# Column means of an 8192 x 8192 matrix: the first pairs added whole, the last accumulation in parts, another order of matmuls and stores

## The chip, the core and the metric

The kernel runs on one core of a Trainium2 chip. The metric is the device time of one execution in microseconds, as a median over runs. Five engines matter. VectorE (DVE in the profile) adds, TensorE (PE) multiplies matrices, ScalarE (ACT) copies and issues some stores, GpSimd (POOL) sets constants, and SyncE (SP) issues the loads. Data moves between the chip's main memory (HBM) and the on-chip memory (SBUF) through 16 DMA engines. TensorE writes its sums into PSUM banks.

## The reference

```python
def setup_inputs():
    return {"x": np.random.randn(8192, 8192).astype(np.float32)}

def reference(x):
    return np.mean(x, axis=0)
```

The input is 268 MB and the output 32 KB. Every input element is read once and added into its column.

## The kernel before

The 8192 rows are cut into 64 groups of 128 rows. A group fills one buffer of 128 partitions by 8192 columns (`P` = 128, `N` = 8192). There are six such buffers in one tile, `bufs` (L29). Buffers 0 to 3 take loads; buffer 4 is called `both` and holds the sum of one pair of groups; buffer 5 is called `acc` and is the accumulator.

Groups are loaded in pairs, 8 MB per load (`load_rows`, L64). Each partition takes two neighbouring rows, so that one lies in buffer `u` and the other in `u + 1`. Group numbers below name a pair by its first group: "group 6" is the pair 6 and 7. Group 0 is loaded straight into `both` and `acc`. Groups 2, 6, 10 and so on go into buffers 0 and 1, groups 4, 8, 12 and so on into buffers 2 and 3 (`u = (g + 2) % 4`). Load 6 therefore has to wait until VectorE has read group 2, and load 8 until it has read group 4.

All loads are issued by SyncE in the order of the program (`load`, L50). A load's issue waits for the adds that read its buffers.

VectorE sums the groups. `add` (L69) issues one addition. Where an add needs a load, a no-op on ScalarE or GpSimd waits for the load and for the add before, and the add waits for the no-op (L74). The first add puts group 0 together (L85). In the loop from L87, each pair takes two adds of 8192 columns:

```python
    for g in range(2, G - 4, 2):
        u = (g + 2) % 4
        dma = load_rows(g, u, 2)
        add(both, bufs[:, u, :], bufs[:, u + 1, :], [dma])
        add(acc, acc, both, [])
```

The first of them is the only one that reads the loaded buffers. Group 60 is added straight into `acc` in three parts of the columns, 8, 4 and 4 blocks of 512 columns, with two adds to each part (L95 to L99).

Groups 62 and 63 are not added by VectorE. Group 62 is loaded in one piece (L101) and group 63 in four (L103), and TensorE reads them. `blocks` (L107) lists matmuls, one for each 512 columns of a row of blocks: `acc`, `r62` (group 62) and `r63` (group 63) are each multiplied with a matrix of ones over 8192, so that the 128 partitions are summed and the results of all three are added up in PSUM. Blocks 0 to 14 fill four banks, four blocks to a bank and three in the last; block 15 goes in four pieces into `last`. The calls from L116 to L123 set the order.

At the end ScalarE copies the four banks to `res` (a part of `both`), VectorE copies `last` to `tail` (L146), and three stores write the output: `s0` for banks 0 to 2 (issued by SyncE), `s3` for bank 3 (issued by ScalarE), and one for `tail` (issued by SyncE). `landed` (L44) makes SyncE wait for what it is given: ahead of `s0` for the waiters' no-ops, ahead of the last store for the loads, the fourth copy and the last matmul, and at the end for the stores.

Of the kernel before, what the change touches and what calls it, by code (L numbers as in the profile page):

```python
# [1 line left out]

# [4 lines left out]


@with_exitstack
def kernel(  # L10
    ctx: ExitStack,
    tc: tile.TileContext,
    x: bass.AP,
    out: bass.AP,
):
    nc = tc.nc
    f32 = mybir.dt.float32
    M, N = x.shape
    P = nc.NUM_PARTITIONS
    F = 512  # L20
    W = F // 4
    G = M // P
    U = 6
    sync = mybir.DependencyInfo(mybir.DependencyClass.Sync, mybir.DependencyReason.DATA)

    sb = ctx.enter_context(tc.tile_pool(name="sb", bufs=1))
    psp = ctx.enter_context(tc.tile_pool(name="psum", bufs=1, space=bass.MemoryType.PSUM))

    bufs = sb.tile([P, U, N], f32, name="bufs")  # L29
    both = bufs[:, U - 2, :]  # L30
    acc = bufs[:, U - 1, :]
    ones = sb.tile([P, 32], f32, name="ones")
    tail = sb.tile([P, W], f32, name="tail")
    warm = sb.tile([P, 32], f32, name="warm")
    nc.gpsimd.memset(ones[:], 1.0 / M)  # L35
    ready = sb.tile([P, 1], f32, name="ready")
    set_up = tc.keep_in_program_order(
        nc.gpsimd.tensor_add(out=ready[:], in0=ones[:, 0:1], in1=ones[:, 1:2])).ins  # L38
    banks = [psp.tile([P, F], f32, name=f"bank{b}") for b in range(4)]
    last = psp.tile([P, W], f32, name="last")  # L40

    loads = []

    def landed(*inss):  # L44

        nop = tc.keep_in_program_order(nc.sync.nop()).ins
        for o in inss:
            tc.add_manual_dep(nop, o.name, sync, reason="SyncE waits")

    def load(dst, src):  # L50
        ins = tc.keep_in_program_order(nc.sync.dma_start(out=dst, in_=src)).ins
        k = len(loads)
        over = loads[k - 8:k - 6] if k >= 8 and k % 2 == 0 else []
        tc.declare_no_dep(ins, group="loads", keep=over, reason="the reader of the buffer waited")
        for o in over:
            tc.add_manual_dep(ins, o.name, sync, reason="covers the next load too")
        tc.add_to_no_dep_group("loads", ins)
        loads.append(ins)
        return ins

    def rows(g, n=1):
        return x[g * P:(g + n) * P, :]

    def load_rows(g, u, n):  # L64
        return load(bufs[:, u:u + n, :], rows(g, n).rearrange("(p j) c -> p j c", j=n))

    adds, joins = [], {}

    def add(dst, a, b, dmas):  # L69

        ins = tc.keep_in_program_order(nc.vector.tensor_add(out=dst, in0=a, in1=b)).ins  # L71
        if dmas and adds:
            waiter = nc.scalar if len(adds) % 8 > 1 else nc.gpsimd
            nop = joins[waiter] = tc.keep_in_program_order(waiter.nop()).ins  # L74
            for o in dmas + adds[-1:]:
                tc.add_manual_dep(nop, o.name, sync, reason="the no-op waits")
            for group in ("loads", "adds"):
                tc.declare_no_dep(ins, group=group, reason="the no-op waited")
            tc.add_manual_dep(ins, nop.name, sync, reason="waits for both at once")
        elif adds:  # L80
            tc.declare_no_dep(ins, group="loads", reason="the add ahead waited")
        tc.add_to_no_dep_group("adds", ins)
        adds.append(ins)

    add(acc, acc, both, [load_rows(0, U - 2, 2)])  # L85
    tc.keep_in_program_order(nc.scalar.copy(out=warm[:], in_=ones[:]))  # L86
    for g in range(2, G - 4, 2):  # L87
        u = (g + 2) % 4
        dma = load_rows(g, u, 2)
        add(both, bufs[:, u, :], bufs[:, u + 1, :], [dma])  # L90
        add(acc, acc, both, [])

    u = (G - 4 + 2) % 4
    dma = [load_rows(G - 4, u, 2)]
    for lo, hi in [(0, 8), (8, 12), (12, 16)]:  # L95
        cols = slice(lo * F, hi * F)
        for j in range(2):
            add(acc[:, cols], acc[:, cols], bufs[:, u + j, cols], dma)
            dma = []  # L99
    r62, r63 = [bufs[:, 2 - u + j, :] for j in range(2)]  # L100
    load(r62, rows(G - 2))  # L101
    for lo, hi in [(0, 8), (8, 12), (12, 15), (15, 16)]:
        load(r63[:, lo * F:hi * F], rows(G - 1)[:, lo * F:hi * F])  # L103

    sums = []

    def blocks(row, lo, hi):  # L107
        for i in range(lo, hi):
            if i < 15:
                sums.append((banks[i // 4], i % 4, row[:, i * F:(i + 1) * F]))  # L110
            else:
                for q in range(4):
                    at = i * F + q * W
                    sums.append((last, q, row[:, at:at + W]))

    blocks(acc, 0, 8)  # L116
    blocks(r62, 0, 16)
    blocks(acc, 8, 12)
    blocks(r63, 0, 8)
    blocks(r63, 8, 12)  # L120
    blocks(acc, 12, 16)
    blocks(r63, 12, 15)
    blocks(r63, 15, 16)  # L123
    for n, (dst, q, cols) in enumerate(sums):
        summed = tc.keep_in_program_order(nc.tensor.matmul(  # L125
            out=dst[32 * q:32 * q + 32, :],
            lhsT=ones[:],
            rhs=cols,
            start=all((d is dst, k) != (True, q) for d, k, _ in sums[:n]),
            stop=all((d is dst, k) != (True, q) for d, k, _ in sums[n + 1:]),  # L130
            tile_position=(0, 32 * q),
            skip_group_check=True,
        )).ins

    res = both[:, :4 * F].rearrange("p (b c) -> p b c", b=4)

    def copy(dst, src):
        return tc.keep_in_program_order(nc.scalar.copy(out=dst, in_=src)).ins  # L138

    def store(engine, dst, src):  # L140
        return tc.keep_in_program_order(engine.dma_start(out=dst, in_=src)).ins

    for b in range(3):
        copy(res[:, b, :], banks[b][:])
    copied = copy(res[:96, 3, :], banks[3][:96])
    ended = nc.vector.tensor_copy(out=tail[:], in_=last[:]).ins  # L146
    landed(*joins.values())
    s0 = store(nc.sync, out[:12 * F].rearrange("(b q c) -> q b c", q=4, c=F), res[0:P:32, 0:3, :])
    s3 = store(nc.scalar, out[12 * F:15 * F].rearrange("(q c) -> q c", q=3), res[0:96:32, 3, :])
    landed(loads[-5], set_up)  # L150
    landed(*loads[-4:-2])
    landed(loads[-2], copied)
    landed(loads[-1], summed)
    store(nc.sync, out[15 * F:].rearrange("(q c) -> q c", q=4), tail[0:P:32, :])
    landed(s0, ended)
    landed(s3)
    hold = tc.keep_in_program_order(nc.vector.nop()).ins
    tc.add_manual_dep(hold, s0.name, sync, reason="VectorE ends late")


# [1 line left out]
_INS = ['x']  # L162
_OUTS = [((8192,), 'float32')]


# [23 lines left out]
```

## Time and profile before

| | us |
|---|---|
| median of three runs | 631.38 (631.07 to 631.54) |
| the profiled execution | 631.49 |
| its span, first to last instruction | 629.6 |
| VectorE busy | 531.0 |
| TensorE busy | 13.1 |
| HBM read over the span | 268.44 MB, 426 GB/s |

A line of the timeline has the start in us, the busy time, the engine, the source line, the operation, its output and input tiles with their shapes, how many there were, and in brackets how long the engine was idle before and what released it. "SPq" and "ACTq" are the queues of instructions of SyncE and ScalarE that are not counted as busy, such as issuing a transfer. "PEld" is the loading of weights into TensorE. A line of the chain of waits has a start, a duration and what it was. A line of the windows has the stretch, its length, the busy time and number of instructions of TensorE, weight loads, VectorE, ScalarE and GpSimd, then TensorE's granted clock, the DMA engines' busy share, and GB/s.

### The profile page before, as it was taken

To read this page: it belongs to the slowest core of one execution; us is meant where nothing else is said; L and a number is where in the kernel's file an instruction comes from. 1 tells how busy PE (TensorE), PEld (TensorE's weight loads), DVE (VectorE), ACT (ScalarE), POOL (GpSimd) and SP (SyncE) were. 2 spreads that over 40 slices of the span, in tenths; PEclk is the share of its full clock that TensorE was granted. 3 is DMA by queue.
4 is the path that set the end of the run, shared out by engine and by line. 5 is a ranking of instruction groups with operands and counts; after the bars stand their busy time and mean duration, and the time that the engine had idled before them with its cause. 6 is when DMAs were issued, how large, how long until landed. Compare 5 with 4: busy or idle time off the path is not lost.

```text
span 629.6 us, 442 instructions
## 1 busy us (share of the span) xinstructions
PE 13.1 (2%) x114; PEld 4.9 (1%) x114; DVE 531.0 (84%) x66; ACT 3.8 (1%) x6; POOL 0.5 (0%) x6
## 2 busy tenths in 40 slices
PE   0000000000000000000000000000000000000007
PEld 0000000000000000000000000000000000000002
DVE  0538988889988889888898888998888988889885
ACT  0000000000000000000000000000000000000001
POOL 0000000000000000000000000000000000000000
PEclk9999999999999999999999999999999999999999
DMA  9999999999999999999999999999999999999995
GB/s 400 408 458 421 446 441 425 446 421 454 412 454 412 454 412 458 408 462 404 462 404 462 404 462 404 462 404 462 404 463 404 462 404 462 404 462 404 462 392 214
DMA packets 5216, 268.50 MB, mean 426 GB/s; under 512 B 587, under 2 KB 591, under 8 KB 862
## 3 DMA queue, kind: packets, MB, share of 16 engines
q1 hardware_dynamic: 5208, 268.46, 98.7%
q8 instruction: 1, 0.02, 0.0%
q10 hardware_dynamic: 6, 0.01, 0.0%
q14 instruction: 1, 0.01, 0.0%
HBM read 268.44 MB, written 0.03 MB: 426 GB/s over the span
## 4 chain that ended last, share of the span: by engine, by line
DMA 67%; DVE 21%; another core or an unknown queue 9%; PE 2%; ACT 0%; issue 0%; ACTq 0%
DMA bufs<-in_x_dram 67%; DVE bufs L71 21%; PE bank L125 2%; ACT L86 0%; PE last L125 0%; ACT bufs L138 0%; ACTq L74 0%; ACT warm L86 0%
## 5 line engine op out<-in xcount | busy, mean ns | idle before, releaser
L71 DVE TENSOR_TENSOR bufs<-bufs 128x8192 f32<-128x8192 f32 (+2 forms) x65 | 530.7, 8167 | 91.4 <-ACTq L74 43.3
L125 PE MATMUL bank<-bufs,ones 128*32 128x512 f32 x90 | 12.8, 687 | 613.1 <-DVE bufs L71 613.1
L125 PEld LDWEIGHTS bank<-bufs,ones 128*32 128x32 f32 x90 | 4.2, 125 | 619.3 <-issue 618.2
L138 ACT COPY bufs<-bank 128x512 f32<-128x512 f32 (+1 forms) x4 | 2.3, 584 | 622.0 <-DMA bufs<-in_x_dram 620.2
L146 DVE COPY tail<-last 128x128 f32<-128x128 f32 x1 | 0.3, 292 | 4.2 <-PE bank L125 4.2
L125 PE MATMUL last<-bufs,ones 128*32 128x128 f32 x24 | 2.3, 276 | 0.0
L86 ACT ACT_TABLE_LOAD x1 | 1.3, 1283 | 0.7 <-PEq L173 0.7
L125 PEld LDWEIGHTS last<-bufs,ones 128*32 128x32 f32 x24 | 1.2, 110 | 1.7 <-issue 1.7
L86 ACT COPY warm<-ones 128x32 f32<-128x32 f32 x1 | 0.2, 218 | 0.0
L38 POOL TENSOR_TENSOR ready<-ones 128x1 f32<-128x1 f32 x1 | 0.2, 193 | 0.1
L35 POOL MEMSET ones<- 128x32 f32 x1 | 0.1, 124 | 0.3 <-POOLq L173 0.3
L173 POOL MEMSET const-bfloat16-1.0<- 128x1 bf16 x1 | 0.1, 101 | 0.0
L173 POOL MEMSET const-uint8-127<- 128x1 uint8 x1 | 0.1, 101 | 0.0
L173 POOL MEMSET const-float32-0.0<- 128x1 f32 x1 | 0.1, 98 | 0.2 <-issue 0.2
L173 POOL MEMSET const-float32-1.0<- 128x1 f32 x1 | 0.1, 98 | 0.0
## 6 DMA issues: line engine op xcount, KB each, us to landing
bufs<-in_x_dram SPq DMA_DIRECT2D x1, 4096.0 KB, 20.3
bufs<-in_x_dram SPq DMA_DIRECT2D x1, 2048.0 KB, 24.7
bufs<-in_x_dram SPq DMA_DIRECT2D x1, 1024.0 KB, 26.8
bufs<-in_x_dram SPq DMA_DIRECT2D x1, 768.0 KB, 28.2
bufs<-in_x_dram SPq DMA_DIRECT2D x31, 29.9
bufs<-in_x_dram SPq DMA_DIRECT2D x1, 256.0 KB, 28.4
out_dram<-bufs SPq DMA_DIRECT2D x1, 24.0 KB
out_dram<-bufs ACTq DMA_DIRECT2D x1, 6.0 KB
```

What stands on the lines that cost most here:

```text
L35: nc.gpsimd.memset(ones[:], 1.0 / M)
L38: nc.gpsimd.tensor_add(out=ready[:], in0=ones[:, 0:1], in1=ones[:, 1:2])).ins
L71: ins = tc.keep_in_program_order(nc.vector.tensor_add(out=dst, in0=a, in1=b)).ins
L86: tc.keep_in_program_order(nc.scalar.copy(out=warm[:], in_=ones[:]))
L125: summed = tc.keep_in_program_order(nc.tensor.matmul(out=dst[32 * q:32 * q + 32, :], lhsT=ones[:], rhs=cols, start=all((d is dst, k) != (T ...
L138: return tc.keep_in_program_order(nc.scalar.copy(out=dst, in_=src)).ins
L146: ended = nc.vector.tensor_copy(out=tail[:], in_=last[:]).ins
L173: nc = _bacc.Bacc("TRN2", target_bir_lowering=False, num_devices=1)
```

## The change

Four things change. For groups 2 to 10 there is one add of 16384 columns per pair: group `g` goes into `both` and `acc`, one row of the pair into each. The separate add of group 0 goes; the first of these adds waits for group 0 too. At group 12, `both` is added into `acc` once, and from there on the loop is as it was. Group 60 is first added up in `both`, in one add of 8192 columns, and `both` is then added into `acc` in three parts. TensorE takes group 62 first, then half of `acc`, half of group 63, and so on. The first store is issued by ScalarE, between its third and fourth copy, and the store of bank 3 directly after the fourth.

```diff
     def add(dst, a, b, dmas):
...
-        if dmas and adds:
+        if dmas:
             waiter = nc.scalar if len(adds) % 8 > 1 else nc.gpsimd
...
-    add(acc, acc, both, [load_rows(0, U - 2, 2)])
+    sums2 = bufs[:, U - 2:, :]
+    first = [load_rows(0, U - 2, 2)]
     tc.keep_in_program_order(nc.scalar.copy(out=warm[:], in_=ones[:]))
     for g in range(2, G - 4, 2):
         u = (g + 2) % 4
         dma = load_rows(g, u, 2)
+        if g < 12:
+            add(sums2, sums2, bufs[:, u:u + 2, :], [dma] + first)
+            first = []
+            continue
+        if g == 12:
+            add(acc, acc, both, [])
         add(both, bufs[:, u, :], bufs[:, u + 1, :], [dma])
         add(acc, acc, both, [])
 
     u = (G - 4 + 2) % 4
-    dma = [load_rows(G - 4, u, 2)]
+    dma = load_rows(G - 4, u, 2)
+    add(both, bufs[:, u, :], bufs[:, u + 1, :], [dma])
     for lo, hi in [(0, 8), (8, 12), (12, 16)]:
         cols = slice(lo * F, hi * F)
-        for j in range(2):
-            add(acc[:, cols], acc[:, cols], bufs[:, u + j, cols], dma)
-            dma = []
+        add(acc[:, cols], acc[:, cols], both[:, cols], [])
...
+    blocks(r62, 0, 16)
     blocks(acc, 0, 8)
-    blocks(r62, 0, 16)
+    blocks(r63, 0, 8)
     blocks(acc, 8, 12)
-    blocks(r63, 0, 8)
     blocks(r63, 8, 12)
     blocks(acc, 12, 16)
...
     for b in range(3):
         copy(res[:, b, :], banks[b][:])
+    s0 = store(nc.scalar, out[:12 * F].rearrange("(b q c) -> q b c", q=4, c=F), res[0:P:32, 0:3, :])
     copied = copy(res[:96, 3, :], banks[3][:96])
+    s3 = store(nc.scalar, out[12 * F:15 * F].rearrange("(q c) -> q c", q=3), res[0:96:32, 3, :])
     ended = nc.vector.tensor_copy(out=tail[:], in_=last[:]).ins
     landed(*joins.values())
-    s0 = store(nc.sync, out[:12 * F].rearrange("(b q c) -> q b c", q=4, c=F), res[0:P:32, 0:3, :])
-    s3 = store(nc.scalar, out[12 * F:15 * F].rearrange("(q c) -> q c", q=3), res[0:96:32, 3, :])
```

## The prediction

> **What bounds the kernel now.** I read the page first: which unit is busy, and how many bytes move.
>
> ```profile
> PE 13.1 (2%) x114; PEld 4.9 (1%) x114; DVE 531.0 (84%) x66; ACT 3.8 (1%) x6; POOL 0.5 (0%) x6
> HBM read 268.44 MB, written 0.03 MB: 426 GB/s over the span
> bufs<-in_x_dram SPq DMA_DIRECT2D x1, 4096.0 KB, 20.3
> ```
>
> VectorE is busy for 84%, but the loads are nearly the whole span. The timeline of the first stretch shows who waits for whom.
>
> ```profile
> 0.74 127.87 SPq L51 DMA_DIRECT2D bufs<-in_x_dram  x8
> 22.79 8.69 DVE L71 TENSOR_TENSOR bufs<-bufs 128x8192 f32<-128x8192 f32 x1 [22.79 <-DMA bufs<-in_x_dram]
> 42.15 17.42 DVE L71 TENSOR_TENSOR bufs<-bufs 128x8192 f32<-128x8192 f32 x2 [10.68 <-POOLq L74]
> 61.51 17.42 DVE L71 TENSOR_TENSOR bufs<-bufs 128x8192 f32<-128x8192 f32 x2 [1.94 <-ACTq L74]
> 80.85 17.42 DVE L71 TENSOR_TENSOR bufs<-bufs 128x8192 f32<-128x8192 f32 x2 [1.93 <-ACTq L74]
> ```
>
> Pairs land every 19.35 us (61.51 minus 42.15, 80.85 minus 61.51); VectorE adds for 17.42 and waits 1.93 for data. The chain of waits says when a buffer comes free:
>
> ```profile
> 61.45 0.04 ACTq L74
> 61.51 8.70 DVE bufs L71
> 70.21 0.02 issue
> 70.23 29.93 DMA bufs<-in_x_dram
> 100.15 0.03 ACTq L74
> ```
>
> Group 4 lands at 61.45. Its pair add ends at 70.21, and 0.03 later group 8 is issued into the same buffers. Group 6 is then still arriving until about 80.80, so the queue has 10.6 us of work left when the next load joins it: that is the cover. In windows of half a microsecond packets are counted where they begin:
>
> ```profile
> 1.50:2.00 0.50, 0.00 (x0) 0.00 (x0) 0.00 (x0) 0.50 (x1) 0.00 (x0) 1.00 5.11 1704
> 60.00:60.50 0.50, 0.00 (x0) 0.00 (x0) 0.00 (x0) 0.00 (x0) 0.00 (x0) 1.00 0.61 262
> 60.50:61.00 0.50, 0.00 (x0) 0.00 (x0) 0.00 (x0) 0.00 (x0) 0.00 (x0) 1.00 3.94 1704
> 61.00:61.50 0.50, 0.00 (x0) 0.00 (x0) 0.00 (x0) 0.00 (x0) 0.00 (x0) 1.00 0.30 131
> ```
>
> The first load, issued at 0.74, begins its packets from 1.50 on. Group 6's packets begin on the different DMA engines between 60.0 and 61.5, around the landing of group 4. The end of the span, from the timeline:
>
> ```profile
> 604.15 17.94 DVE L71 TENSOR_TENSOR bufs<-bufs 128x4096 f32<-128x4096 f32 x6 [1.94 <-ACTq L74]
> 613.13 6.84 PE L125 MATMUL bank<-bufs,ones 128*32 128x512 f32 x43 [613.13 <-DVE bufs L71]
> 616.52 0.22 PEld L125 LDWEIGHTS bank<-bufs,ones 128*32 128x32 f32 x4 [0.63 <-issue]
> 617.22 0.14 PEld L125 LDWEIGHTS bank<-bufs,ones 128*32 128x32 f32 x4 [0.48 <-issue]
> 624.13 0.58 ACT L138 COPY bufs<-bank 128x512 f32<-128x512 f32 x1 [0.27 <-PE bank L125]
> 626.05 0.58 ACT L138 COPY bufs<-bank 96x512 f32<-96x512 f32 x1 [1.33 <-PE bank L125]
> 626.66 1.28 ACTq L141 DMA_DIRECT2D out_dram<-bufs  x1
> 626.91 0.56 SPq L141 DMA_DIRECT2D out_dram<-tail  x1
> ```
>
> TensorE starts at 613.13, when the accumulator's first half is done, and the chain of waits shows it without a gap to 626.02. The last load, issued at 595.31, lands 28.4 later (DMA issues), at 623.7, before its matmuls from 625.4 on. So the last 16 us are TensorE, a copy, and the last stores. That a piece of work starts later here is paid in full.
>
> **Part 1: five pairs added whole.** For groups 2 to 10 one add of 128x16384 replaces two of 128x8192. From the forms, 2048 columns take 2.289 us, 4096 take 4.426, 8192 take 8.692: 1.0415 ns a column and 0.16 fixed, so 17.22 for 16384. VectorE has 58 adds in place of 65 and some 1.1 us less to do. Worth nothing: the 1.93 us wait for each pair hides it. The first add now waits on GpSimd's no-op for groups 0 and 2 together and starts at 42.15, where the add of group 2 starts already. The add of group 0 at 22.79 released no buffer, so its absence costs nothing as long as VectorE keeps up.
>
> What costs is the release. Buffers of groups 2 to 10 come free after 17.22 us, not 8.69, so loads 6 to 14 are issued 8.53 later: group 6 at 42.15+17.22+0.03 = 59.40, not 50.87. That is 2.05 ahead of 61.45, not 10.6. SyncE's queue holds nothing else behind these waits than the next load. Is 2.05 enough? If the queue were quite empty, the load would take what the first one took from issue to its add, 22.79-0.74 = 22.05: its add at 81.45 against 80.85, 0.60 late. If all start-up lay beside the packets still running, 0. The packets of the late load can begin from 59.40+0.76 = 60.16 (first row of the windows, at the earliest), and most DMA engines have run dry by 61.0, so for them it is a start from empty; the slowest is still at work to 61.07 or so. I take 0.5, near the first load's row. An upper end: from the issue of the last store, 626.91, the windows show no packet before 628.0, 1.1 to 1.6 later against 0.76 to 1.26; 0.35 more would make it 0.95.
>
> It isn't paid five times. Group 8 is issued at 61.51+17.22+0.03 = 78.76; from empty its add is at 100.81. Behind group 6, itself 0.60 late, it is at 80.85+0.60+19.35 = 100.80: nothing further. Group 10 is issued 17.3 after the late landing of 6 and meets the old gap again. So groups 6, 10 and 14 pay, 8 and 12 don't: 3 x 0.5 = 1.5 us (0 to 2.9).
>
> At group 12 the extra add of both into acc (8.69) comes first. With L the landing of group 10, VectorE ends that add at L+26.0, the pair add of 12 at L+34.7, and load 16 is issued 4.0 ahead of the landing of 14 at L+38.7. Above 2.05+0.60 = 2.65 nothing is lost. Each later pair gains the 1.93, so the old cover is back after four pairs.
>
> One rule of the Trainium skill speaks for less. "DMA: Bandwidth & Descriptors", section "Latency and other measured facts", gives about 600 ns to the first byte of a load issued by SyncE; the first row of the windows has 0.76 at the least. By the page the packets could begin at 60.00, before any engine is dry, the stall would be near 0 and the sum 632.3.
>
> **Part 2: the accumulator in parts.** After group 60 lands, six adds (17.94) become one of 8.69 and three of 4.43, 2.29, 2.29: 17.76 with gaps, ending at 621.91 for 622.09. But the first half is ready at 617.3, not 613.04. TensorE's new order hides that.
>
> **Part 3: group 62 first.** Its load is issued at 593.51 and lands 20.3 later, at 613.81. TensorE so starts near 613.87, not 613.13: 0.74 later. Does it run through? Warm, four matmul passes side by side take 0.43, before 617 they take 0.85 (the rows at 616.52 and 617.22 are where it changes). A row of groups is eight such steps and 0.22: 3.66; the slow start adds 1.97; three rows give 12.95, near the 12.89 seen. Group 62 is done at 613.87+3.66+1.97 = 619.5, after the first half at 617.3; the second part (619.6) is wanted at 622.9, the last (621.91) at 624.6. No stall, so 0.74 goes to the end, with the last stores behind it. If the slow start is a matter of time since the start, it's the same after. I can't see that in one execution: half of every microsecond that it is longer or shorter is the price, and I allow 0.5 either way.
>
> In the rows the slow stretch lasts 3.7, from 613.13 to about 616.8. The Trainium skill, "TensorE: Matmul & The Clock Gate", section "Part 1: The HAM clock gate", says that the change comes at the end of a window of about 3.4 us that runs freely, so that the slow stretch varies. By the page's 500 ns either way the sum would move by 0.25.
>
> **Part 4: stores on ScalarE.** The first store leaves SyncE (0.69 there at 624.74) and stands between the third and the fourth copy. Queued behind it are the fourth copy, the second store, and SyncE's wait for that copy, behind which the last store waits. Room: the third copy ends at 624.71, the fourth begins at 626.05, 1.34 us. ScalarE's only store issue took 1.28; this one has 12 rows of 2 KB, not 3, and on SyncE 12 rows took 0.69 where four took 0.56. I take 1.28+0.13 = 1.41, and with two gaps of 0.03 the fourth copy is 0.13 late; 0 if it takes 0.69; 0.7 if it doubles by its first use. The second store may issue faster, but the last store on SyncE starts 0.25 later than it and goes out later; a gain there ends nothing.
>
> **Sum.** 1.5 + 0.74 + 0.13 = 2.4. The profiled execution took 631.49 on a span of 629.6, 1.9 outside it: 633.9, span 632.0. It stands 0.11 above the median, so the forecast is 631.38+2.4 = 633.8.
>
> **Rivals.**
> (a) The late loads' start-up is hidden by packets still under way, the slowest engine above all, and only the tail costs 0.74 to 0.87: 632.2, not measurably slower. For it: packets begin up to 61.5, after 60.16. Against: most begin before 61.0, and need a read under way. It decides where first packets come before each engine has run dry, about 60.0 to 61.0.
> (b) A start from empty costs 0.95, as the stores' delay suggests: 2.9+0.87, 635.1. Against: loads have their own row.
> (c) TensorE's slow stretch, or ScalarE's store, adds up to 0.7 to the forecast: 634.5.
> (d) Faster: the slow stretch is 3 us shorter as TensorE starts at another moment (-1.5), the stall is hidden, and the rest is 0.87: 630.7. It decides only above 1.7 us shorter without any stall; nothing in the rows shows it.
>
> **How the numbers follow.** About 0.2%, 1.26 us, is what can be told from no change. Forecast 0.46 (own range 632.9 to 634.5), (a) 0.22, (b) 0.17, (c) 0.12, (d) 0.03. Slower by over 0.2% (above 632.64): the forecast, (b) and (c) with a little of (a), 0.76; same 0.21; faster 0.03. Range 631.9 to 635.5, leaving out the far ends of (a), (b), (d).
>
> **What would show it.** Part 1: five adds of about 17.2 from 42.15 on; the adds of groups 6, 10 and 14 start 19.35 plus 0.3 to 0.6 after the ones before, those of 8 and 12 at 19.35. Then 19.35 throughout. Part 3: first matmul 9.7 after group 60's add starts, not 9.0, and no gap. Part 4: the fourth copy begins within 0.2 of the last bank matmul. Wrong if group 6's add starts at 80.85, if the gap comes with every one of the five loads, or if the wait for the accumulator shows on TensorE.

## The result: slower by 1.0%

The changed kernel took 637.80 us (median of four, 637.10 to 638.84) where the kernel before took 631.46 (631.07 to 631.54): a ratio of 1.0103, with a 95% interval of 1.0085 to 1.0120. That is 6.3 us, where 2.4 were forecast and the range ended 4 us up. The direction was right, the size was not.

The profiled execution after the change is the slowest of its four (638.84, span 637.0). These are the lines of its page that answer to those of before:

```profile
PE 13.2 (2%) x114; PEld 5.4 (1%) x114; DVE 529.8 (83%) x59; ACT 3.8 (1%) x6; POOL 0.5 (0%) x6
HBM read 268.44 MB, written 0.03 MB: 421 GB/s over the span
bufs<-in_x_dram SPq DMA_DIRECT2D x1, 4096.0 KB, 20.3
```

VectorE has the forecast's 1 us less to do, and the loads run at 421 GB/s instead of 426. The timeline of the first stretch shows where:

```profile
42.18 17.23 DVE L71 TENSOR_TENSOR bufs<-bufs 128x16384 f32<-128x16384 f32 x1 [42.18 <-POOLq L74]
62.07 17.23 DVE L71 TENSOR_TENSOR bufs<-bufs 128x16384 f32<-128x16384 f32 x1 [2.67 <-POOLq L74]
82.56 17.23 DVE L71 TENSOR_TENSOR bufs<-bufs 128x16384 f32<-128x16384 f32 x1 [3.27 <-ACTq L74]
103.32 17.23 DVE L71 TENSOR_TENSOR bufs<-bufs 128x16384 f32<-128x16384 f32 x1 [3.53 <-ACTq L74]
123.30 61.00 DVE L71 TENSOR_TENSOR bufs<-bufs 128x16384 f32<-128x16384 f32 x6 [2.76 <-ACTq L74]
184.80 17.42 DVE L71 TENSOR_TENSOR bufs<-bufs 128x8192 f32<-128x8192 f32 x2 [0.49 <-ACTq L74]
```

The whole add takes 17.23 as forecast. But the distances between adds are 19.89, 20.49, 20.76 and 19.98 in place of 19.35, and from 123.30 to 184.80 three pairs take 61.50 in place of 58.05. Together this is 7.2 us, all of it before 185. Afterwards pairs come every 19.35 again. The chain of waits has the transfers themselves in the place of the cover:

```profile
59.41 0.02 issue
59.43 23.07 DMA bufs<-in_x_dram
82.50 0.04 ACTq L74
```

Group 6 was issued at 59.43 (forecast: 59.40) and took 23.07 to land. The first load of all, which found empty queues, needed about 22.0 before the change. Group 4 had landed at 62.01, 2.6 us after that issue. A load issued behind 2.6 us of remaining work was thus slower than one issued behind none.

The end of the span after the change, from the timeline:

```profile
610.51 17.55 DVE L71 TENSOR_TENSOR bufs<-bufs 128x8192 f32<-128x8192 f32 x4 [1.93 <-ACTq L74]
620.32 5.29 PE L131 MATMUL bank<-bufs,ones 128*32 128x512 f32 x27 [620.32 <-DMA bufs<-in_x_dram]
631.47 0.58 ACT L144 COPY bufs<-bank 128x512 f32<-128x512 f32 x1 [1.13 <-PE bank L131]
632.09 1.18 ACTq L147 DMA_DIRECT2D out_dram<-bufs  x1
633.39 0.58 ACT L144 COPY bufs<-bank 96x512 f32<-96x512 f32 x1 [1.33 <-PE bank L131]
634.00 0.75 ACTq L147 DMA_DIRECT2D out_dram<-bufs  x1
634.25 0.63 SPq L147 DMA_DIRECT2D out_dram<-tail  x1
```

The first add of group 60 starts at 610.51 for 604.15: 6.36 of the 7.40 us by which the spans differ lie ahead of it. (That is less than the 7.2 seen by 185, because before the change one landing, near 469, came 0.8 late.) From that add to the end it is 26.49 for 25.45, so 1.04 is the tail. The first matmul comes 9.81 after the add, not 8.98.

### The profile page after: what moved, and what is told of

It reads as the page before. It is cut to its first block, busy times and chain, and to the rows that moved or that the text cites. A ratio compares the mean times of both kernels' runs of the same rounds, so it can differ in the third digit from the quotient of the medians.

```text
span 637.0 us, 434 instructions
## 1 busy us (share of the span) xinstructions
PE 13.2 (2%) x114; PEld 5.4 (1%) x114; DVE 529.8 (83%) x59; ACT 3.8 (1%) x6; POOL 0.5 (0%) x6
## 2 busy tenths in 40 slices
DMA packets 5216, 268.50 MB, mean 422 GB/s; under 512 B 587, under 2 KB 591, under 8 KB 862
## 4 chain that ended last, share of the span: by engine, by line
DMA 68%; DVE 29%; PE 2%; issue 0%; ACT 0%; SPq 0%; ACTq 0%; POOLq 0%
DMA bufs<-in_x_dram 68%; DVE bufs L71 29%; PE bank L131 2%; PE last L131 0%; ACT bufs L144 0%; SPq L51 0%; ACTq L74 0%; POOLq L74 0%
## 5 line engine op out<-in xcount | busy, mean ns | idle before, releaser
L71 DVE TENSOR_TENSOR bufs<-bufs 128x8192 f32<-128x8192 f32 (+3 forms) x58 | 529.6, 9133 | 98.5 <-POOLq L74 54.6
```

## The experiments

### Which part costs what

Two kernels take the change apart. The first is the kernel before with the whole adds of the diff and nothing else of it; the second is the changed kernel with the old loop.

```diff
     for g in range(2, G - 4, 2):
         u = (g + 2) % 4
         dma = load_rows(g, u, 2)
+        if g < 12:
+            add(sums2, sums2, bufs[:, u:u + 2, :], [dma] + first)
...
```

```diff
-        if g < 12:
-            add(sums2, sums2, bufs[:, u:u + 2, :], [dma] + first)
-            first = []
-            continue
-        if g == 12:
-            add(acc, acc, both, [])
         add(both, bufs[:, u, :], bufs[:, u + 1, :], [dma])
         add(acc, acc, both, [])
```

> The kernel before with part 1 alone (five whole adds). Forecast's theory: three starved loads at 0.5 each, +1.5, so 632.9. Theory A (late release, dearer than forecast): all of the loss but the tail's 1.0 is here, +5.3 us, about 636.7, and the waits of VectorE grow at groups 6 to 14, not at every second one. Theory B (the whole adds themselves slow the transfers): the same time, but packets are slow while a whole add runs, in group 4's load already.

> The changed kernel with part 1 undone (accumulator in parts, group 62 first, ScalarE's two stores stay). Forecast: +0.87 us, TensorE starting 0.74 later against group 60's first add, ScalarE's store 0.13. Rival: ScalarE's first store delays the fourth copy by 0.7, then +1.4. If the loss of 6.3 us is in the tail after all, +5 or more.

Part 1 alone took 637.79 against 631.32 (ratio 1.0100, 1.0084 to 1.0116): all the loss, within the uncertainty. The tail alone took 632.26, so +0.94 (ratio 1.0015, 1.0006 to 1.0024), where 0.87 were forecast. The forecast's +1.5 for part 1 falls. In this profile of part 1 alone the adds stand so:

```profile
42.02 17.23 DVE L71 TENSOR_TENSOR bufs<-bufs 128x16384 f32<-128x16384 f32 x1 [42.02 <-POOLq L74]
61.42 17.23 DVE L71 TENSOR_TENSOR bufs<-bufs 128x16384 f32<-128x16384 f32 x1 [2.17 <-POOLq L74]
83.48 17.23 DVE L71 TENSOR_TENSOR bufs<-bufs 128x16384 f32<-128x16384 f32 x1 [4.84 <-ACTq L74]
102.85 17.23 DVE L71 TENSOR_TENSOR bufs<-bufs 128x16384 f32<-128x16384 f32 x1 [2.13 <-ACTq L74]
122.63 78.52 DVE L71 TENSOR_TENSOR bufs<-bufs 128x16384 f32<-128x16384 f32 x8 [2.56 <-ACTq L74]
```

Group 4 is on time (19.40), so theory B's slow packets in its load are not there. Group 6 is 2.71 late, group 8 on time behind it, group 10 late by 0.43; by the landings in the trace group 12 is on time and group 14 late by 2.59, 5.7 in all. The pattern of every second load is the forecast's; the price is not, and in the changed kernel's own profile even the pattern isn't kept.

### Is it the late release, or the long add?

Here no add is longer than before. For groups 2 to 10 the columns are cut at 7840; the accumulator gets its 7840 columns before the pair sum takes the last 352, so the loaded buffers are read to the end only after 17.2 us.

```diff
-        add(both, bufs[:, u, :], bufs[:, u + 1, :], [dma])
-        add(acc, acc, both, [])
+        dmas = [dma]
+        for lo, hi in [(0, 7840), (7840, N)] if g < 12 else [(0, N)]:
+            add(both[:, lo:hi], bufs[:, u, lo:hi], bufs[:, u + 1, lo:hi], dmas)
+            add(acc[:, lo:hi], acc[:, lo:hi], both[:, lo:hi], [])
+            dmas = []
```

> The kernel before, with groups 2 to 10 added in another order: pair sum and accumulator for columns 0 to 7839, then both for the last 352. No whole add, the same VectorE work and 10 more short instructions, but the loaded buffers come free about 17.2 us after the start, as with whole adds. Theory A: the loss of part 1 alone, about +5.3 us. Theory B: no loss, 631.5. Forecast's arithmetic: +1.5.

It took 638.23 (ratio 1.0106, 1.0092 to 1.0120): the whole loss, without any whole add. Theory B falls, and late release is shown to be enough. The timeline shows the three gaps where the forecast had put them:

```profile
61.59 17.68 DVE L71 TENSOR_TENSOR bufs<-bufs 128x7840 f32<-128x7840 f32 x4 [1.66 <-ACTq L74]
83.97 17.68 DVE L71 TENSOR_TENSOR bufs<-bufs 128x7840 f32<-128x7840 f32 x4 [4.71 <-POOLq L74]
103.32 17.68 DVE L71 TENSOR_TENSOR bufs<-bufs 128x7840 f32<-128x7840 f32 x4 [1.66 <-ACTq L74]
123.12 17.68 DVE L71 TENSOR_TENSOR bufs<-bufs 128x7840 f32<-128x7840 f32 x4 [2.12 <-POOLq L74]
142.45 17.42 DVE L71 TENSOR_TENSOR bufs<-bufs 128x8192 f32<-128x8192 f32 x2 [1.66 <-ACTq L74]
164.13 17.42 DVE L71 TENSOR_TENSOR bufs<-bufs 128x8192 f32<-128x8192 f32 x2 [4.26 <-ACTq L74]
```

Distances of 22.38, 19.35, 19.80, 19.33, 21.68: groups 6, 10 and 14 are 3.03, 0.45 and 2.33 late, 5.8 in all; 8 and 12 are on time.

The counter-test keeps the two accumulators but gives the cover back. Each of the five pairs is loaded in two halves and added as two adds.

```diff
+        if g < 12:
+            halves = [load(bufs[:, u + j, :], rows(g, 2).rearrange("(p j) c -> p j c", j=2)[:, j, :]) for j in range(2)]
+            add(both, both, bufs[:, u, :], [halves[0]] + first)
+            add(acc, acc, bufs[:, u + 1, :], [halves[1]])
+            first = []
+            continue
```

> Pairs 2 to 10 go into pair sum and accumulator as in part 1, but as two adds of 8192 columns, and each of these pairs is loaded in two halves of 4 MB, so that one buffer is free after 8.7 us and the other after 17.4, with half a load more in the queue. Theory A: cover is 10 us again and more, no loss, 631.5 within 0.6. If summing into two accumulators or skipping the add of group 0 is itself the cause: +5 us.

It took 632.50 (ratio 1.0014, 1.0005 to 1.0023), 1.2 over the kernel before: not quite nothing, but five of the six us are gone. So neither the two accumulators nor the missing first add costs them. These are lines of its timeline:

```profile
604.63 17.94 DVE L71 TENSOR_TENSOR bufs<-bufs 128x4096 f32<-128x4096 f32 x6 [1.92 <-ACTq L74]
613.62 7.64 PE L133 MATMUL bank<-bufs,ones 128*32 128x512 f32 x43 [613.62 <-DVE bufs L71]
627.33 0.58 ACT L146 COPY bufs<-bank 96x512 f32<-96x512 f32 x1 [1.33 <-PE bank L133]
```

Group 60's first add starts at 604.63, 0.48 later than before, and TensorE's fourth-bank copy starts 13.7 us after the first matmul (627.33 less 613.62), where it was 12.9 before (626.05 less 613.13). The rest is thus a little in the loads and a longer slow stretch of TensorE, not the gaps.

### How the price depends on the lead

Call "lead" the time from a load's issue to the landing of the load before it: 10.6 us before the change, 2.05 in part 1. Two kernels hold the buffers longer at seven pairs only, four apart, each with another lead. For leads of 1, 0 and -2 an add on a spare tile is put ahead of the last columns; it adds nothing to the result. These kernels, and those of the same kind below, ran once each, so that what is read from them are single executions.

```diff
+        cut, extra = {2: (4050, []), 10: (5970, []), 18: (6930, []), 26: (7840, []), 34: (7840, [840]), 42: (7840, [1800]), 50: (7840, [1800, 1800])}.get(g, (N, []))
...
+            if lo:
+                for n in extra:
+                    add(spare[:, :n], spare[:, :n], spare[:, :n], [])
```

> The kernel before; at pairs 2, 10, 18, 26, 34, 42, 50 alone the buffers are held longer, by adding nearly all columns into the accumulator ahead of the last ones (and for the last three by idle adds on a spare tile), so that the load two pairs on is issued 6, 4, 3, 2, 1, 0 and -2 us ahead of the landing before it. Read: by how much that load's add is late. Forecast's arithmetic, 2.65 minus the lead: 0, 0, 0, 0.65, 1.65, 2.65, 4.65. Theory C (a short lead is worth nothing: the DMA engines take up the new load as if it came when they are empty): about 2.7 at 2, 1 and 0, 4.7 at -2, with a threshold above 2. Theory D (an engine that misses its turn loses one packet of 2.4 us): steps of 2.4.

> The same with the leads in the order 0, 2, 4, -2, 1, 6, 3, to tell the lead's effect from that of the place in the run and of the spread among engines that earlier gaps left. All theories: the same value for the same lead as in the other order, within 0.5; if not, the state left by the earlier gaps matters.

The lateness of the add two pairs on, worked out from the starts of the adds less 19.35 (at leads of 0 and -2, where VectorE is itself behind, from the held pair's own add less two periods):

| lead | forecast's arithmetic | first order | second order |
|---|---|---|---|
| 6 | 0 | 0.00 | 0.00 |
| 4 | 0 | 0.00 | 0.92 |
| 3 | 0 | 0.62 | 0.00 |
| 2 | 0.65 | 2.39 | 1.73 |
| 1 | 1.65 | 1.30 | 0.44 |
| 0 | 2.65 | 2.51 | 2.47 |
| -2 | 4.65 | 4.43 | 4.39 |

At 0 and below, where the DMA engines are empty, the forecast's arithmetic holds within 0.3. It fails at a lead of 2, and there the price is above that at a lead of 1. Theory C's flat 2.7 falls at the lead of 1.

Values at 1, 3 and 4 differ between the orders by more than 0.5. At 1 this is not the lead's doing. In the second order the load ahead (of group 36) landed late by itself, so the lead came out as 2.13 and not 1:

```profile
361.31 16.69 DVE L73 TENSOR_TENSOR bufs<-bufs 128x7840 f32<-128x7840 f32 x2 [1.91 <-ACTq L76]
381.59 17.42 DVE L73 TENSOR_TENSOR bufs<-bufs 128x8192 f32<-128x8192 f32 x2 [1.66 <-POOLq L76]
401.38 17.42 DVE L73 TENSOR_TENSOR bufs<-bufs 128x8192 f32<-128x8192 f32 x2 [2.37 <-ACTq L76]
```

The distances are 20.28 and 19.79, so the two adds together are 1.37 late, near the 1.30 of the first order. Single landings that are 0.5 to 0.9 late although their load was issued 10 us or more ahead stand in 11 of the 14 profiled executions of this case. The kernel before has one:

```profile
448.52 17.42 DVE L71 TENSOR_TENSOR bufs<-bufs 128x8192 f32<-128x8192 f32 x2 [1.92 <-ACTq L74]
468.68 17.42 DVE L71 TENSOR_TENSOR bufs<-bufs 128x8192 f32<-128x8192 f32 x2 [2.73 <-ACTq L74]
```

The 0.62 at a lead of 3 and the 0.92 at 4 can't be told from these; that a lead of 3 or 4 costs anything is not shown.

To have the same gap several times from a fresh state, two more kernels put a gap with a lead of -2 between any two with a lead of 2, or of 1. The diff is that for 2; for 1, each `(7840, [])` is `(7840, [840])`.

```diff
+        cut, extra = {2: (7840, []), 10: (7840, [1800, 1800]), 18: (7840, []), 26: (7840, [1800, 1800]), 34: (7840, []), 42: (7840, [1800, 1800]), 50: (7840, [])}.get(g, (N, []))
```

> The kernel before with buffers held longer at seven pairs only, spaced four apart: at pairs 2, 18, 34, 50 so that the load two pairs on is issued 2 us ahead of the landing before it, at pairs 10, 26, 42 so that it is issued 2 us after that landing (which sets the DMA engines level again). Packets of 64 KB. Forecast's arithmetic: 0.65 late at each lead of 2, 4.65 at each of -2. Theory D (engines that stay busy past the issue fall behind by up to one packet, 2.4 us): 0.65 to 3.0 at a lead of 2, 1.5 to 2.7 in the mean, and the spread of the engines' last packets grows to about 2.4; 4.5 at -2.

> The same with a lead of 1 us at pairs 2, 18, 34, 50. Forecast's arithmetic: 1.65 late. Theory D: an engine that is dry when the load comes starts at once and one that is busy falls behind; with a spread of 0.7 nearly all are dry by the time the load arrives, so 1.4 to 1.8, less than at a lead of 2.

With a lead of 2 the four were 1.83, 1.58, 1.98 and 1.55 late, with a lead of 1 they were 1.33, 1.32, 1.08 and 1.28. In the trace the leads came out as 2.13 to 2.15, and as 1.19 to 1.40, for which the forecast's arithmetic gives 0.5, and 1.25 to 1.46. So it holds within 0.2 at a lead of 1 and is missed by 1.0 to 1.5 at a lead of 2, and the order of the two is turned round. From issue to landing the four loads with a lead of 1 took 21.83 to 21.88, like those with a lead of -2 in the same kernel (21.78 to 22.03); the four with a lead of 2 took 23.04 to 23.47. The first of each, in the timelines (the lines of the issue and of VectorE's adds of groups 4 and 6); lead 2, whose load was issued at 59.12:

```profile
59.12 0.33 SPq L53 DMA_DIRECT2D bufs<-in_x_dram  x1
61.31 17.42 DVE L73 TENSOR_TENSOR bufs<-bufs 128x8192 f32<-128x8192 f32 x2 [1.66 <-ACTq L76]
82.49 17.42 DVE L73 TENSOR_TENSOR bufs<-bufs 128x8192 f32<-128x8192 f32 x2 [3.76 <-ACTq L76]
```

and lead 1, issued at 60.19:

```profile
60.19 0.33 SPq L53 DMA_DIRECT2D bufs<-in_x_dram  x1
61.45 17.42 DVE L73 TENSOR_TENSOR bufs<-bufs 128x8192 f32<-128x8192 f32 x2 [0.72 <-ACTq L76]
82.13 17.42 DVE L73 TENSOR_TENSOR bufs<-bufs 128x8192 f32<-128x8192 f32 x2 [3.27 <-POOLq L76]
```

Issued 1.07 us later, the load is there 0.36 earlier. The windows of half a microsecond, in which a packet counts where it begins (the last number is GB/s), show the difference. With a lead of 2:

```profile
60.00:60.50 0.50, 0.00 (x0) 0.00 (x0) 0.00 (x0) 0.00 (x0) 0.00 (x0) 1.00 0.42 131
60.50:61.00 0.50, 0.00 (x0) 0.00 (x0) 0.00 (x0) 0.00 (x0) 0.00 (x0) 1.00 1.90 655
61.00:61.50 0.50, 0.00 (x0) 0.00 (x0) 0.19 (x1) 0.00 (x0) 0.00 (x0) 1.00 1.75 655
61.50:62.00 0.50, 0.00 (x0) 0.00 (x0) 0.50 (x1) 0.00 (x0) 0.00 (x0) 1.00 1.46 524
62.00:62.50 0.50, 0.00 (x0) 0.00 (x0) 0.50 (x1) 0.00 (x0) 0.00 (x0) 1.00 0.37 131
```

and with a lead of 1:

```profile
60.50:61.00 0.50, 0.00 (x0) 0.00 (x0) 0.22 (x1) 0.00 (x0) 0.00 (x0) 1.00 0.01 0
61.00:61.50 0.50, 0.00 (x0) 0.00 (x0) 0.05 (x1) 0.00 (x0) 0.00 (x0) 1.00 5.56 1835
61.50:62.00 0.50, 0.00 (x0) 0.00 (x0) 0.50 (x1) 0.00 (x0) 0.00 (x0) 1.00 0.72 262
```

Sixteen packets of 64 KB are 2097 GB/s in such a row. With a lead of 1, all 16 began within one microsecond, 0.8 to 1.8 after the issue. With a lead of 2 the first packets trickle in over two, the last of them about 3 us after the issue, although the load before had landed by 61.3.

At both issues all 16 engines were still at their last packets of the load before. The trace's records of single packets give the times. With a lead of 1 those last packets end between 60.34 and 61.03, and the new load's first ones begin between 61.15 and 61.67, 0.96 to 1.48 after the issue. With a lead of 2 they end between 60.33 and 60.89, and the new ones begin between 60.47 and 62.17, 1.35 to 3.05 after the issue. So at least one engine stood idle for 1.28 us or more, though the new load had been issued before it ran dry. In both cases the first packets take longer than the 2.42 us of later ones (3.14 and 2.94 in the mean), as they do in the very first load (3.15 in the kernel before).

### Is it the size of a packet?

Theory D was that an engine that misses its turn loses one packet. Packets of 32 KB should then halve the extra.

```diff
-        return load(bufs[:, u:u + n, :], rows(g, n).rearrange("(p j) c -> p j c", j=n))
+        return load(bufs[:, u:u + n, :], rows(g, n).rearrange("(j p) c -> p j c", j=n))
```

The same change goes into part 1 alone and into the kernel with four leads of 2. A third kernel describes each row as two halves:

```diff
+        return load(bufs[:, u:u + n, :].rearrange("p j (h c) -> p (j h) c", h=2),
+                    rows(g, n).rearrange("(p j) (h c) -> p (j h) c", j=n, h=2))
```

> Part 1 alone, but every pair load takes rows p and 128+p into partition p, in packets of 32 KB and not 64 KB. Theory D: the loss per gap halves with the packet, about +3 us in place of +6. Theory C and the forecast's arithmetic: no change of the loss, about +6 (or +1.5 by the forecast).

> As the first, with packets of 32 KB (rows p and 128+p into partition p). Theory D: what goes beyond 0.65 halves, 0.65 to 1.9 in all, and the spread stays under 1.3. If the extra has to do with the transfers under way and not with the packet: as with 64 KB.

> As the first, with each row described in two halves of 16 KB (if they go out as one packet, it repeats the first). Theory D: 0.65 to 1.3, spread under 0.7 plus what was there.

Part 1 with 32 KB packets took 637.79 (ratio 1.0097, 1.0083 to 1.0111), as with 64 KB. Pairs then come every 19.43 undisturbed, 0.08 more, which is some 2 us over the whole run (worked out, as no kernel with 32 KB packets and the old release was run). By the landings its groups 6 to 14 are 0.28, 0, 1.40, 0.36 and 2.24 late, 4.3 in all, where part 1 alone had 5.7: less, but not half. In the kernel with four leads of 2 the adds were late by 0.12, 2.78, 0.14 and 3.15, in the mean 1.55. The attempt at 16 KB went out in the old 64 KB packets (5216 packets in all, as before) and is a repetition: 2.40, 1.13, 2.12, 1.65. All eight with 64 KB have a mean of 1.78. The mean does not halve with the packet, and two of the four with 32 KB lie above the theory's own upper end of 1.9: theory D is not borne out.

### TensorE's slow stretch

The forecast took the first 3.7 us of matmuls, at half the rate, to be a matter of the time since TensorE's start. Ten idle matmuls into a spare bank, released by the first add of group 60, test that on the kernel before.

```diff
+    for k in range(10):
+        q = k % 4
+        spun = tc.keep_in_program_order(nc.tensor.matmul(
+            out=spin[32 * q:32 * q + 32, :], lhsT=ones[:], rhs=idle[:], start=True, stop=True,
+            tile_position=(0, 32 * q), skip_group_check=True)).ins
+        if k == 0:
+            tc.add_manual_dep(spun, adds[-6].name, sync, reason="starts with the last adds")
```

> The kernel before, and ten idle matmuls into a spare bank on TensorE from the end of the first add of group 60 on (608.6), ahead of the real ones at 613.1. If the slow stretch belongs to the first 3.7 us of TensorE's work, the real matmuls run fast from the start and end some 1.9 us earlier, up to the last load's landing at 623.7: about -1.7 us, 629.6. If it is tied to something else, no change.

It took 629.84 against 631.39: ratio 0.9975 (0.9965 to 0.9985), faster than both kernels by 1.5 and 8 us. In its timeline:

```profile
608.83 4.48 PE L129 MATMUL spin<-idle,ones 128*32 128x512 f32 x20 [608.83 <-DVE bufs L74]
613.19 4.92 PE L135 MATMUL bank<-bufs,ones 128*32 128x512 f32 x43
624.44 0.58 ACT L148 COPY bufs<-bank 96x512 f32<-96x512 f32 x1 [1.38 <-PE bank L135]
```

The 43 matmuls that took 6.84 before now take 4.92, and the fourth copy comes 11.25 after the first real matmul, not 12.92. The slow stretch belongs to the start of TensorE's work, as assumed. The trace's record of TensorE's granted clock says the same: its first entry, the full clock, is at 617.06 in the kernel before, 3.92 us after the first matmul, and here at 612.32, 3.49 us after the first idle one and 0.87 ahead of the first real one. The Trainium skill, "TensorE: Matmul & The Clock Gate", section "Why this matters for your kernels", advises at least 4 us of warming up ahead of a measurement. In this execution the 4.4 us from the first idle matmul to the first real one were enough; in the 13 kernels without idle matmuls the entry comes 3.5 to 5.5 us after the first matmul, so they need not always be.

## Why the prediction was wrong, and where it was right

**The step that failed** is in part 1: "I take 0.5, near the first load's row", with 0 and 0.95 as ends. The term made of it, 3 x 0.5 = 1.5 us (0 to 2.9), measured 6.5 in part 1 alone. One gap at a lead of 2 measured 1.1 to 2.4, with a mean of 1.8 over eight, and up to 3.0 in the late-release kernel. The bounds were drawn from one thought: that a load issued early can at worst do as badly as one issued to empty queues. The first load was the only start that the trace showed, and it is a start from empty. The runs at leads of 1 and 2 show that a load issued while the engines' last packets have 1.2 to 1.8 us to run (issue 59.12) can land later than one issued when they have 0.1 to 0.9 to run (issue 60.19).

Why that is so stays open. It is shown that the first packets then begin over 2 us and not 1, with engines idle in between, and that halving the packet doesn't halve the loss. What delays these engines was not isolated.

**How often it is paid.** "Groups 6, 10 and 14 pay, 8 and 12 don't" held in the late-release kernel (3.03, 0, 0.45, 0, 2.33) and in part 1 alone (2.71, 0, 0.43, 0, 2.59), if with unlike prices. It did not hold in the changed kernel's profiled execution, where groups 4 to 14 are 0.54, 1.14, 1.41, 0.63, 2.79 and 0.67 late (the last two by the landings). There the gap came with every one of the five loads, which the prediction had named as a sign of being wrong. The sums are 5.8, 5.7 and 7.2.

The pattern was worked out from landings, that is, from the last of the 16 engines. The trace has a completion for each of them, and a late load sets them apart: in the changed kernel the 16 completions of a load lie 0.74 apart for group 4, 1.54 for group 6, 2.34 for group 8 and 3.39 for group 12. So group 8's load, issued at 79.32, came 3.2 us ahead of the last completion of group 6 but only 1.65 ahead of the first. In part 1 alone, group 10's load was issued at 100.74, when the first engine had been done with group 8 since 100.62; it took 21.83, no more than a start from empty, and was 0.43 late. That this spread decides which loads pay fits these numbers but was not tested by itself.

Group 4's load was issued before any release was late; its 0.54 isn't in the profile of part 1 alone, and I have no cause for it, but it is of the size of the single late landings that most executions have.

**The return of the cover** fits: group 16's add waited only 0.49 for its load, since VectorE was still behind, and group 18's stands 19.34 after it. No gap shows from there on.

**The whole adds** were right to 0.01 us (17.22 forecast, 17.23 measured), as was their issue at 59.40 (59.43).

**The rule of the skill** on the first byte ("DMA: Bandwidth & Descriptors", "Latency and other measured facts", about 600 ns) would have made the stall vanish. The trace contradicts that use of it: in the kernel with a lead of 1 the first packet begins 0.96 us after the start of the issue (0.63 after the issuing instruction's 0.33 us are over, so the figure itself is near), but with a lead of 2 the last one begins about 3 us after it, and the load lands with its last engine. In the first load of the kernel before, the packets begin 1.01 to 1.41 us after the issue; the prediction's 0.76 was the edge of a window. The measurement decides.

**The tail**: 0.87 forecast, 1.04 in the profile, +0.94 in the experiment. Of it, TensorE's later start was forecast at 0.74 and measured 0.83 (9.81 less 8.98). ScalarE's store was forecast at 0.13 and measured 0: it took 1.18, not 1.41, and the fourth copy began at 633.39, 13.07 after the first matmul against 12.92 before, with the bank's last matmul as its releaser. The 0.15 between these is TensorE's own longer run: its clock record begins 4.24 us after the first matmul, not 3.92, and of a longer slow stretch half is lost. The second store took 0.75 instead of 1.28 and gained nothing, since the last store of SyncE goes out after it, as forecast.

**The rivals.** Rival (b), a dearer start, was the right direction and too small: 0.95 a gap, 635.1. Rival (a), a hidden start, falls with every gap at a lead of 2 and 64 KB packets. Of (d), a shorter slow stretch, nothing was seen in the changed kernel. The chance of 0.76 for slower was on the right side; the range of 635.5 was too tight at its upper end.

## What to carry to other kernels

When a change eats into the lead with which a transfer is issued, don't take the remaining lead as credit: here a lead of 6 us was free, what 3 and 4 cost stays within the scatter, and one of 2 cost more, in the mean, than one of 1. Price a buffer's release by the instruction that reads it last: two adds of 8.7 that free a buffer after the first are worth more than one of 17.2 with the same work. And if a short burst of matmuls sets the end of a kernel, idle matmuls in the 4 to 5 us ahead of it can shorten it.

## What the runs showed of the hardware that was not expected

A load issued 1.07 us later landed 0.36 us earlier (issue 60.19, add at 82.13; issue 59.12, add at 82.49). The window rows give TensorE's granted clock as 1.00 throughout, also where the matmuls ran at half the rate. The clock record behind that column has no entry before 617.06 in the kernel before, so its 1.00 ahead of that isn't a reading; the spacing of weight loads shows the slow stretch (0.85 us for four, then 0.43). And the slow stretch differs between executions: the clock record's first entry came 3.92 us after the first matmul before the change, 4.24 after it, and 5.53 in the kernel with halved loads. From the first matmul to the fourth copy it was 12.92 us, 13.07 and 13.71, with the same number of matmuls: half of the difference.
